# One more quantum between copy and transposes in two key chains of the second mixer, and one more quantum of projection ahead of its first scores

## The chip, the cores and the metric

The kernel runs on one core of a Trainium2 chip. TensorE (PE) does matmuls and transposes, VectorE (DVE), ScalarE (ACT) and GpSimd (POOL) the elementwise work, and SyncE (SP) issues the transfers. Each engine works through its own queue in order. The metric is the device time of one execution in microseconds, as the median of several runs.

## The reference, cut to what matters

The reference is a decoder trunk of two layers on 256 tokens of width 1024. Layer 0 has a mixer of a state-space part and a short convolution, layer 1 a mixer of attention; each layer ends in a mixture of experts. The change is in layer 1's mixer, of which this is the part that matters:

```python
proj = rms_norm(h) @ w_in                       # 2340 columns
qm, km, vm, qd, kc, vc, ks, vs, kw, vw, gl = split(proj)
# MoBA: 4 heads, one block of 256 keys: causal attention of qm on km, vm
# NSA: 12 heads in 2 groups, three branches on the queries qd:
k_cmp = rms_norm(compress_blocks(kc, ...))      # blocks of 32 tokens, stride 16: 15 keys
v_cmp = compress_blocks(vc, ...)                # gelu(flat @ w1) @ w2
o_c = softmax(qd @ k_cmp) @ v_cmp               # compressed branch
o_s = softmax(qd @ ks) @ vs                     # selected branch
o_w = softmax(qd @ kw) @ vw                     # window branch
o_nsa = g[0] * o_c + g[1] * o_s + g[2] * o_w
out = concat(o_moba, o_nsa) @ w_out
```

With 256 tokens all blocks are selected and the window holds every token.

## The kernel before

The order of the work on each engine is written out by hand: an instruction stands in its engine's queue where the program emits it. The function `odd` is the second mixer.

**The projection.** It is cut into nine pieces of 256 (one of 292) columns, and each piece into four quanta of 12 matmuls, numbered here q0 to q35 in the order in which they are emitted. Pieces come in the order 0, 1, 3, 2, 4, 5, 7, 6, 8. A quantum needs its weights as a high and a low half, made two quanta ahead by `prep`: ACT copies the high half (L211), and DVE or POOL, as the string `OD_SPLIT` says, subtracts to get the low half (L212; POOL for q14, q15, q18 to q20 and from q23 on). The first four matmuls of a quantum need the high half alone, the next four the low half.

**The jobs.** When a piece is done, a generator for it is appended to `jobs`: `blocks(0)` behind q3, `keys(1)` behind q7, `queries(3)` behind q11, `plain_values(2)` behind q15, `queries(4)` behind q19, and so on. `quantum()` emits one quantum (while there are some) and then calls `work()`, which moves each job on by one `yield`. So a `yield` in a job is a distance of one quantum in the queues.

- `blocks(0)` has ACT copy the raw compressed keys and values, scaled by `rs`, to `kd` (L962); at the next step it transposes them on PE (L969) and DVE adds the position terms into `fl` (L974).
- `keys` and `queries` begin with `head_rms`: squares on ACT (L868), the sum `hss` on DVE (L869), a chain of 16 small operations on POOL to `hrs` (L870 to L872), and some quanta later `hn` on DVE (L887 or L916), transposes on PE (L895 or L923) and the split results `kS`, `kmS` or `qS` (L901 and L902, L926 and L928).
- `compressed` follows 64 matmuls (L1172) on `fl`, in which `work()` is called four times: gelu (L978), transposes (L982), a matmul (L987), then a chain on POOL to `crs`; after two yields DVE makes `kn` (L995), after one more PE transposes it (L998) and spreads the values (L1001), and DVE and ACT finish `kcS` and `vpad` (L1005 to L1008). Then it goes on as `batch(3)`, whose scores are L1030, with L1033 and L1034 on DVE behind them.

**The attention.** It has 22 units u. A loop over i from -3 to 22 emits in this order: T(i), S(i+3), C(i+1), M(i+3), E(i+2), Q, V(i-1), D. S are the scores (L1091, L1094), M the maxima on DVE (L1100), E the exponentials on ACT (L1107), C the scaling on DVE (L1115 to L1126), T the transposes of probabilities (L1133, copied by L1134), V the values (L1154, L1160) with the split of the result into `yh` and `yl` (L211, L212). Units 0 to 17 are six groups of three, of which the middle one has no V; units 18 to 21 have two each. Q is one quantum (three in i = -3), and only a call of `work()` once all 36 are emitted. D is one unit of the output projection (L407, its weights L397 and L398): eight units are emitted in this half, the n-th of them after V has finished group n. The output projection is created at the end of the first iteration in which all quanta are emitted and no job is left.

Ahead of this loop q0 to q2 are emitted with the transposes of the input, then `quanta(9)` emits q3 to q11, then come the matmuls L1172, and `quanta(4)` emits q12 to q15. The three quanta of i = -3 are q16 to q18, and q35 is in i = 14.

Of the kernel before, what the change touches and what calls it, by code (L numbers as in the profile page):

```python
# [65 lines left out]
def tile_trunk(ctx: ExitStack, tc: tile.TileContext, x, cst, sml, s5c, ev_w_in, ev_w_out, od_w_in, od_w_out,  # L66
# [9 lines left out]
    def ps(tag, shape, dt=F32):  # L76
        return psum.tile(shape, dt, name=tag, tag=tag, bufs={"acc": 3, "mm": 2, "tp": 2, "o": 1}[tag])
# [15 lines left out]
    def cs(n):  # L93
        o, w = _CST[n]
        return C[:, o:o + w]
# [74 lines left out]
    def rsq2(pool, y, v, shape, eng=None):  # L170

        e = eng or ve
        t = [pool.tile(list(shape), F32, name=f"rsq{i}_{len(shape)}_{shape[-1]}", bufs=2) for i in range(2)]
        e.tensor_scalar(y.bitcast(I32), v.bitcast(I32), -0.5, MAGIC, op0=OP.mult, op1=OP.add)
        e.tensor_scalar(t[0], v, -0.5, None, op0=OP.mult)
        for _ in range(3):
            e.tensor_tensor(t[1], y, y, op=OP.mult)
            e.tensor_tensor(t[1], t[1], t[0], op=OP.mult)
            if eng:
                e.tensor_scalar(t[1], t[1], 1.5, None, op0=OP.add)  # L180
                e.tensor_tensor(y, t[1], y, op=OP.mult)
            else:
                e.scalar_tensor_tensor(y, t[1], 1.5, y, op0=OP.add, op1=OP.mult)
# [595 lines left out]
    def odd():  # L779
        with tc.tile_pool(name="odd", bufs=1, reuse_waits="tile") as sp:  # L780
# [39 lines left out]
            def quantum():  # L820
                nonlocal nq
                if nq < 36:
                    q, nq = nq, nq + 1
                    i, c0 = order[q // 4], 2 * (q % 4)
                    prep(q + 2)
                    n = pieces[i][2]
                    if c0 == 0:
                        if n > 256:
                            acc[i] = [ps("acc", [P, 512])[:, :n] for _ in range(2)]
                        else:  # L830
                            p = ps("mm", [P, 2, 256])
                            acc[i] = [p[:, t] for t in range(2)]
                    wh, wl = W.pop(q)
                    for m, (a, b) in enumerate(((xh, wh), (xh, wl), (xl, wh))):
                        for k in range(2):
                            for t in range(2):
                                pe.matmul(acc[i][t], a[:, c0 + k, t * P:(t + 1) * P], b[:, k],  # L837
                                          start=(c0 + k == 0 and m == 0 and (n > 256 or t == 0)),
                                          stop=(c0 + k == 7 and m == 2), skip_group_check=True)
                    if c0 == 6:  # L840
                        jobs.append(after[i])
                work()

            def quanta(n):
                for _ in range(n):
                    quantum()
# [113 lines left out]
            def blocks(i):  # L960
                for t in range(2):
                    ac.activation(kd[:, t], heads(acc[i][t])[:, :, None, :].to_broadcast([P, 4, 2, 64]), AF.Copy,  # L962
                                  scale=rs[:, t:t + 1])
                yield
                for i in range(2):
                    p = ps("tp", [P, 2, 2, P])
                    for hd in range(2):
                        for t in range(2):
                            pe.transpose(p[:, hd, t], kd[:, t, 2 * i + hd].rearrange("p a d -> p (a d)"), ident)  # L969
                    for r in range(2):  # L970
                        v = p[half[r]]
                        iv = bass.AP(tensor=v.tensor, offset=v.offset + r, ap=[v.ap[0], [2, 16], [256, 2], [16, 15]])
                        o = fl[half[r], i].rearrange("p s (h n) -> p s h n", h=2)[:, :, :, 0:15]
                        tt(o, iv, pev[half[r], i, :, None, None].to_broadcast([64, 16, 2, 15]), op=OP.add)  # L974
                    yield

            def compressed(ph):
                ac.activation(hid, ph, AF.Gelu_apprx_tanh)  # L978
                yield
                p = ps("tp", [P, 2, P])  # L980
                for c in range(2):
                    pe.transpose(p[:, c], hid[:, c * P:(c + 1) * P], ident)  # L982
                ve.tensor_copy(hT, p)
                yield
                p = ps("tp", [P, P])
                for c in range(2):
                    pe.matmul(p, hT[:, c], w2c[:, c].rearrange("p i n -> p (i n)"), start=(c == 0), stop=(c == 1))  # L987
                ac.activation(kc, p, AF.Copy)
                css, crs, sq = T("css", (P, 1)), T("crs", (P, 1)), T("csq", (P, 64), tag="hn", bufs=3)
                ac.activation(sq, p[:, 0:64], AF.Square, accum_out=css)  # L990
                po.tensor_scalar(css, css, 1.0 / 64, EPS, op0=OP.mult, op1=OP.add)
                rsq2(sp, crs, css, (P, 1), po)
                for _ in range(2):
                    yield
                ts(kn, kc[0:64, None, 0:64].to_broadcast([64, 2, 64]), crs[0:64], None, op0=OP.mult)  # L995
                yield
                p = ps("tp", [P, 512])
                pe.transpose(p[:, 0:64], kn.rearrange("p c d -> p (c d)"), ident[0:64, 0:64])  # L998
                rep = cs("rep").rearrange("p (h m) -> p h m", h=2)
                for hd in range(2):  # L1000
                    pe.matmul(p[0:96, 128 + 128 * hd:256 + 128 * hd], rep[:, hd], kc, start=True, stop=True,  # L1001
                              skip_group_check=True)
                v = p[:, 0:64].rearrange("p (h n) -> p h n", h=2)[:, :, 0:16]
                o = kcS[:, 0:64].rearrange("p (h m n) -> p h m n", h=2, m=2)
                ac.activation(o[:, :, 0], v, AF.Copy, scale=gkc)  # L1005
                stt(o[:, :, 1], v, gkc, o[:, :, 0].bitcast(F32), op0=OP.mult, op1=OP.subtract)
                for hd in range(2):
                    tt(vpad[:, hd], p[0:96, None, 192 + 128 * hd:256 + 128 * hd].to_broadcast([96, 6, 64]),  # L1008
                       cs("bm")[0:96, :, None].to_broadcast([96, 6, 64]), op=OP.mult)
                yield  # L1010
                yield from batch(3)
# [125 lines left out]
            def values(u):  # L1137
# [19 lines left out]
                if t == 1:  # L1157
# [6 lines left out]
                    ready.add(g)  # L1164

            after.update({0: blocks(0), 1: keys(1), 7: keys(7), 2: plain_values(2), 8: plain_values(8)})
            after.update({i: queries(i) for i in (3, 4, 5, 6)})
            quanta(9)
            ph = ps("o", [P, 256])
            for j in range(16):  # L1170
# [3 lines left out]
                if j % 4 == 3:  # L1174
                    work()
            jobs.append(compressed(ph))
            quanta(4)
            yh = big.tile([P, 8, 256], F32R, name="yh")
            yl = big.tile([P, 8, 256], F32R, name="yl")
            dense, nd = None, 0  # L1180
# [443 lines left out]
    even()  # L1624
    moe(0, False)
    odd()
    moe(1, True)

# [94 lines left out]
```

## Time and profile before

| | |
|---|---|
| median of 3 runs | 515.37 us (514.63 to 515.45) |
| profiled execution, its own time | 516.22 us |
| its span, first to last instruction | 514.6 us |
| busy: PE / DVE / ACT / POOL | 483.6 / 293.4 / 212.7 / 138.4 us |
| mean granted clock of PE, share of full speed | 0.991 |
| second mixer in the trace | about 244 to 387 us |

The profile is of one execution. Busy times add up instructions of an engine, overlapping ones once. A line of a timeline has the start in us, the duration in us of so many merged instructions, engine, line of the program, operation, tiles (written <- read), shapes, the count, and in brackets the idle time ahead of it with what ended it.

### The profile page before, as it was taken

How to read it: one execution, taken by the hardware profiler on the slowest of the kernel's cores; microseconds unless marked ns; L12 is line 12 of the kernel's file. 1: busy time of each engine (PE TensorE's matmuls, PEld its weight loads, DVE VectorE, ACT ScalarE, POOL GpSimd, SP SyncE). 2: the span in 40 equal slices, each digit the busy share in tenths (PEclk: the TensorE clock that was granted, in tenths of full speed). 3: DMA queues.
4: the chain of work that ended last, by engine and by line, in shares of the span. 5: the costliest groups of instructions: out<-in, count | busy, mean ns of one | idle time of the engine just before them, and what ended most of it. 6: DMA issues, size and time to landing. Idle time of an engine off the chain costs nothing. (4 is left out here: it accounts for less than half of the span.)

```text
span 514.6 us, 9047 instructions
## 1 busy us (share of the span) xinstructions
PE 483.6 (94%) x3245; PEld 324.7 (63%) x3245; DVE 293.4 (57%) x682; ACT 212.7 (41%) x468; POOL 138.4 (27%) x292
## 2 busy tenths in 40 slices
PE   7998998998989999999899889989998989999996
PEld 5997987786444443535877768877776444443532
DVE  6876678747733333435654687977547732333433
ACT  4636633664231121114645776786654131121211
POOL 6899980001000000010344556651232000000000
PEclk9999997999999999999999999999999999999998
DMA  8948942449599999999939600242059699999952
GB/s 295 406 157 335 405 162 84 144 154 323 179 400 384 358 417 413 419 385 383 317 130 377 222 0 3 91 159 80 1 163 415 265 378 384 348 414 414 407 248 82
DMA packets 36591, 137.63 MB, mean 267 GB/s; under 512 B 4544, under 2 KB 8768, under 8 KB 31424
## 3 DMA queue, kind: packets, MB, share of 16 engines
q1 hardware_dynamic: 36544, 137.03, 70.1%
q8 instruction: 27, 0.44, 0.3%
q14 instruction: 20, 0.16, 0.1%
HBM read 135.70 MB, written 1.05 MB: 266 GB/s over the span
## 5 line engine op out<-in xcount | busy, mean ns | idle before, releaser
L1482 PE MATMUL mm<-slab,xg 128*64 128x512 f32 (+1 forms) x512 | 99.2, 595 | 0.0
L1482 PEld LDWEIGHTS mm<-slab,xg 128*64 128x64 f32 (+1 forms) x512 | 30.5, 130 | 58.3 <-issue 55.4
L212 DVE TENSOR_TENSOR w<-slab,w 128x1024 fp32r<-128x1024 f32 (+2 forms) x39 | 39.9, 1031 | 13.4 <-ACT w L211 12.3
L313 PE MATMUL mm<-xh,w 128*128 128x256 f32 x288 | 41.3, 294 | 3.8 <-DVE yb L372 3.3
L1499 DVE COPY aT<-tp 128x256 f32<-128x256 f32 x14 | 5.9, 424 | 66.9 <-PE tp L1497 66.9
L211 ACT ACTIVATE w<-slab 128x512 fp32r<-128x512 f32 (+2 forms) x57 | 43.3, 780 | 1.3 <-PE mm L837 0.9
L313 PEld LDWEIGHTS mm<-xh,w 128*128 128x128 f32 x288 | 38.2, 201 | 4.1 <-issue 4.1
L837 PE MATMUL mm<-w,xh 128*128 128x256 f32 x256 | 38.6, 293 | 0.2 <-ACT xh L242 0.2
L837 PEld LDWEIGHTS mm<-w,xh 128*128 128x128 f32 x256 | 33.3, 189 | 1.2 <-ACT xh L242 0.9
L1488 ACT ACTIVATE si<-mm,rsl 128x256 f32<-128x256 f32 x14 | 6.7, 475 | 65.0 <-PE mm L1482 64.9
L1523 DVE TENSOR_TENSOR h<-h,acc 128x512 f32<-128x512 f32 x44 | 28.2, 681 | 2.8 <-PE acc L1520 2.8
L1511 PE MATMUL o<-slab,aT 128*64 128x512 f32 (+1 forms) x128 | 27.1, 603 | 1.0 <-DVE aT L1499 1.0
L849 POOL MEMSET fl<- 128x2048 f32 x1 | 1.8, 1804 | 97.1 <-PE tp L1423 97.1
L212 POOL TENSOR_TENSOR w<-slab,w 128x512 fp32r<-128x512 f32 (+1 forms) x18 | 24.0, 1339 | 13.9 <-ACT w L211 9.5
L1429 ACT ACTIVATE xg<-tp,sml 128x256 f32<-128x256 f32 (+1 forms) x32 | 12.6, 444 | 36.0 <-PE tp L1423 36.0
L212 DVE TENSOR_TENSOR ylp<-o,xlp 128x512 fp32r<-128x512 f32 x14 | 9.7, 692 | 30.4 <-ACT xlp L211 30.4
L1511 PE MATMUL acc<-slab,aT 128*64 128x512 f32 (+1 forms) x128 | 26.9, 600 | 0.0
L407 PE MATMUL acc<-w,yh 128*128 128x512 f32 x80 | 25.6, 399 | 0.0
L211 ACT ACTIVATE xlp<-o 128x512 fp32r<-128x512 f32 x14 | 8.4, 598 | 40.1 <-PE acc L1520 27.9
L1423 PEld LDWEIGHTS tp<-Pm,xhm 128*128 128x128 f32 x128 | 16.4, 189 | 11.1 <-issue 4.9
L398 DVE TENSOR_TENSOR w<-slab,w 128x512 fp32r<-128x512 f32 (+1 forms) x18 | 17.1, 964 | 10.4 <-ACT w L397 8.7
L1107 ACT ACTIVATE pr<-acc,mx 128x128 f32<-128x128 f32 (+1 forms) x56 | 22.9, 424 | 0.1
(436 smaller groups left out, 998.6 us busy)
## 6 DMA issues: line engine op xcount, KB each, us to landing
slab<-in_w_gate_dram SPq DMA_DIRECT2D x64, 512.0 KB, 8.1
slab<-in_w_up_dram SPq DMA_DIRECT2D x64, 512.0 KB, 8.9
slab<-in_w_down_dram SPq DMA_DIRECT2D x32, 1024.0 KB, 10.6
slab<-in_ev_w_in_dram SPq DMA_DIRECT2D x8, 1024.0 KB, 14.0
slab<-in_od_w_in_dram SPq DMA_DIRECT2D x8, 1024.0 KB, 6.6
slab<-in_ev_w_out_dram SPq DMA_DIRECT2D x4, 1024.0 KB, 12.3
slab<-in_od_w_out_dram SPq DMA_DIRECT2D x4, 1024.0 KB, 9.2
slab<-in_ev_w_in_dram SPq DMA_DIRECT2D x4, 512.0 KB, 7.5
```

The source lines that it names most:

```text
L211: ac.activation(hi, src, AF.Copy)
L212: (eng or ve).tensor_tensor(lo, src, hi.bitcast(F32), op=OP.subtract)
L313: pe.matmul(p, a[:, c], b[:, c], start=(c == 0 and n == 0), stop=(c == 7 and n == 2))
L398: (po if s.done in s.pool else ve).tensor_tensor(wl, v[:, o:o + s.n], wh.bitcast(F32), op=OP.subtract)
L407: pe.matmul(acc[t, f], a[:, c, t * P:(t + 1) * P], b[:, f * 512:(f + 1) * 512], start=(first and m == 0), stop=(last and m == 2))
L837: pe.matmul(acc[i][t], a[:, c0 + k, t * P:(t + 1) * P], b[:, k], start=(c0 + k == 0 and m == 0 and (n > 256 or t == 0)), stop=(c0 + k == 7 ...
L1107: ac.activation(pr[:, q * nk:(q + 1) * nk], U[u]["s"][:, q * w:q * w + nk], AF.Exp, bias=U[u]["m"][:, q:q + 1], accum_out=su[:, q:q + 1])
L1423: pe.matmul(p[b][:, d], v[:, t, c], Pm[:, t, 256 * g:256 * g + n_], start=(n + d + t == 0), stop=(n + t == 2), skip_group_check=True)
L1429: ac.activation(xgs[g][:, c, :n_], p[b][:, d], AF.Copy, scale=w)
L1482: pe.matmul(p[w * k:w * k + w], xgs[j // 2][:, c, o:o + w], wgu[j][k][c // 4][:, :, c % 4], start=(c == 0), stop=(c == 7), tile_position=( ...
L1511: pe.matmul(py[v], aT[:, c, v], wd[j][k][:, c, f * 512:(f + 1) * 512], start=(c == 0), stop=(c == 1), tile_position=(0, w * k))
L1523: tt(v, v, q[t], op=OP.add)
```

## The change

Three numbers of yields or quanta change, and nothing of the computation. `blocks` yields twice between the `kd` copies and the transposes, so that q5 stands between q4 and the first transposes instead of following them. `compressed` yields three times instead of twice ahead of `kn`. `quanta(5)` emits q12 to q16 ahead of the loop instead of q12 to q15; the three quanta of i = -3 are then q17 to q19, each later quantum stands one iteration of the loop earlier, and q35 is in i = 13.

```diff
@@ blocks
                     ac.activation(kd[:, t], heads(acc[i][t])[:, :, None, :].to_broadcast([P, 4, 2, 64]), AF.Copy,
                                   scale=rs[:, t:t + 1])
                 yield
+                yield
                 for i in range(2):
                     p = ps("tp", [P, 2, 2, P])
@@ compressed
                 rsq2(sp, crs, css, (P, 1), po)
-                for _ in range(2):
+                for _ in range(3):
                     yield
                 ts(kn, kc[0:64, None, 0:64].to_broadcast([64, 2, 64]), crs[0:64], None, op0=OP.mult)
@@ odd
             jobs.append(compressed(ph))
-            quanta(4)
+            quanta(5)
```

## Rows read from the trace of the kernel before

**Rows 1.** The page: busy time, share and instructions of each engine

```profile
PE 483.6 (94%) x3245; PEld 324.7 (63%) x3245; DVE 293.4 (57%) x682; ACT 212.7 (41%) x468; POOL 138.4 (27%) x292
```

**Rows 2.** Table of stretches: length, busy PE, PEld, DVE, ACT, POOL, clock, DMA

```profile
358.00:377.00 19.00, 19.00 (x121) 14.19 (x120) 11.38 (x28) 11.30 (x33) 5.27 (x4) 1.00 0.00 1
```

**Rows 3.** PE's waits, 244 to 377 us: in total, times, longest

```profile
PE tp L1133 <- DVE pr L1122: 1.7, 2, 1.0
PE tp L969 <- ACT early L962: 1.5, 2, 1.3
PE tp L998 <- DVE early L995: 1.4, 1, 1.4
PE tp L1133 <- DVE kmS L902: 1.3, 1, 1.3
PE tp L923 <- DVE hn L916: 1.0, 2, 0.6
...
PE tp L1133 <- DVE pr L1126: 0.6, 1, 0.6
...
PE tp L895 <- DVE hn L887: 0.3, 1, 0.3
```

**Rows 4.** Timeline of PE: the starts of q7 and q8

```profile
256.49 1.11 PE L837 MATMUL mm<-w,xh 128*128 128x256 f32 x8
...
257.91 1.11 PE L837 MATMUL mm<-w,xh 128*128 128x256 f32 x8
```

**Rows 5.** Timelines of ACT, DVE and POOL, 251 to 273 us

```profile
251.49 1.27 ACT L962 ACTIVATE early<-mm,rs 128x512 f32<-128x512 f32 x2 [2.57 <-POOL rs L181]
...
253.31 0.69 DVE L212 TENSOR_TENSOR w<-slab,w 128x512 fp32r<-128x512 f32 x1 [3.03 <-ACT w L211]
253.92 1.32 DVE L974 TENSOR_TENSOR fl<-tp,sml 64x480 f32<-64x480 f32 x2
...
258.98 0.69 DVE L869 TENSOR_REDUCE hss<-sq 128x8 f32<-128x512 f32 x1 [0.34 <-ACT sq L868]
259.58 1.96 DVE L212 TENSOR_TENSOR w<-slab,w 128x512 fp32r<-128x512 f32 x3
...
259.76 0.56 POOL L870 TENSOR_SCALAR hss<-hss 128x8 f32<-128x8 f32 x1 [7.73 <-DVE hss L869]
...
265.13 0.20 POOL L872 TENSOR_TENSOR hrs<-hrs,rs 128x8 f32<-128x8 f32 x1
268.14 0.20 POOL L870 TENSOR_SCALAR hss<-hss 128x8 f32<-128x8 f32 x1 [2.81 <-DVE hss L869]
...
272.38 0.20 POOL L872 TENSOR_TENSOR hrs<-hrs,rs 128x8 f32<-128x8 f32 x1
```

**Rows 6.** Timelines of POOL, DVE and ACT, 285 to 294 us

```profile
285.46 2.49 POOL L212 TENSOR_TENSOR w<-slab,w 128x512 fp32r<-128x512 f32 x2
...
285.54 1.26 DVE L995 TENSOR_SCALAR early<-early,crs 64x128 f32<-64x128 f32 x1 [2.14 <-POOL crs L181]
...
288.66 1.28 ACT L1107 ACT_TABLE_LOAD   x1
...
291.34 0.64 ACT L211 ACTIVATE w<-slab 128x512 fp32r<-128x512 f32 x1
292.59 0.84 ACT L868 ACTIVATE sq<-mm,rs 128x256 f32<-128x256 f32 x2 [0.61 <-PE mm L837]
```

**Rows 7.** Timelines of PE, ACT and DVE around the last values

```profile
373.29 0.66 PE L1154 MATMUL o<-pT,vm 128*64 128x128 f32 x8
373.87 0.50 PE L407 MATMUL mm<-w,yh 128*128 128x512 f32 x1
374.21 0.40 PE L407 MATMUL mm<-w,yl 128*128 128x512 f32 x1
...
373.99 0.39 ACT L211 ACTIVATE yh<-o 128x256 fp32r<-128x256 f32 x1 [1.38 <-PE o L1154]
...
374.41 0.42 DVE L212 TENSOR_TENSOR yl<-o,yh 128x256 fp32r<-128x256 f32 x1 [1.07 <-ACT yh L211]
```

## The prediction

> **What bounds the kernel now.** I read the page first, then the list of PE's waits cut to the second mixer's stretch, then tables of stretches, then the timelines of PE, ACT, DVE and POOL. PE is busy for 94% of the span [rows 1], so what can be won lies in the gaps of PE's in-order queue, and those are few. From 358 to 377 us PE is busy for the whole stretch [rows 2]: there the mixer is set by PE's own work, and any new wait costs its full length. The gaps lie further ahead, and the list of PE's waits names them [rows 3]: 1.5 us in two pieces before the transposes of L969 (for ACT's `kd` copies), 1.4 us before L998 (for DVE's `kn`), 1.7 us in two pieces and 0.6 us before the transposes of probabilities L1133, 1.3 us before one more of those (for `kmS`), 1.0 us in two pieces before L923, and 0.3 us before L895. No matmul is added or removed by the change, so its worth is the sum of these gaps now, less their sum afterwards. One quantum of the projection is 1.42 us of PE, the distance between the starts of two of them [rows 4].
>
> **First edit: a yield more in `blocks`.** Now PE reaches the transposes right after quantum q4, while ACT's `kd` copies start only at 251.49 us and take 1.27 us, because `rs` comes from POOL [rows 5]. With the yield q5 stands between, and its 1.42 us cover nearly all of the 1.5 us. But the mixer does not get these 1.5 us. What is late next is DVE. From 253.31 us its queue holds the low halves of the weights of q6 to q9 and the two pairs of additions L974. In rows: 253.31 to 253.92 is 0.6 for a low half, a pair of L974 is 1.32 [rows 5]; four low halves and two pairs make 4 x 0.65 + 2 x 1.32 = 5.3 us, whatever their order, so that the reduction `hss` of the first keys can start at 253.31 + 5.3 = 258.6 us, against 258.98 now [rows 5]. That is 0.35 us earlier and no more. The start of the queue does not move, since its first low half hangs on ACT's split behind the same `kd` copies. Behind `hss` comes POOL's chain to `hrs`, from 259.76 to 265.33 us [rows 5], then L895, and then the same chain for the first queries (268.14 to 272.58) and L923. PE has waits of 0.3 and 0.4 us there [rows 3], so both are set by that chain, and PE coming earlier only makes them longer. I take 0.35 us. The bounds: 0, if ACT's squares, not DVE, set the start, and 1.5, if the chain shrinks as well.
>
> POOL's first chain takes 5.57 us and the second 4.44 us. The first runs beside three low halves on DVE (from 259.58 us, 1.96 us) and its first operation takes 0.56 us; the same operation of the second takes 0.20 us [rows 5]. The Trainium skill (GPSIMD Engine Reference, section Specifications) says that GpSimd shares its SBUF interfaces with VectorE and is disturbed by VectorE's instructions with two SBUF inputs, and the trace agrees with that. By the order of the queue the low halves of q10 to q12 still follow `hss` directly, so the chain stays at 5.57 us and the term at 0.35; if they fell outside of it, 265.33 would come 1.1 us sooner and the term would be 0.35 + 1.1 = 1.45 us.
>
> **Second edit: three yields before `kn`, and quanta(5).** These belong together. The compressed keys keep their place against the units of attention (`kn` in the first of three quanta of i = -3), and there is one quantum more, q16, between the matmul L987 and `kn`. The 1.44 us before L998 lie between the end of q17 and the end of `kn`, which ran from 285.54 for 1.26 us, after POOL's chain to `crs` [rows 6]. With q18 in between they are covered. What is late next is the low half of q18's weights: POOL starts it at 285.46 us, when the chain is through, and does two in 2.49 us [rows 6], so it is there at 286.7. PE would be at q18 at about 285.5 and do its first four matmuls in 0.5 us, so it waits some 0.75 us for the fifth. Left of 1.4 are 0.65 us. The bounds are 0 (POOL later, or `kn` stretched further) and 1.4.
>
> **Third: the projection is one iteration ahead of the attention.** All jobs of the pieces from the fourth on run one iteration earlier. The squares of `queries(4)` on ACT (L868, 0.84 us) are now at 292.59, after the exponentials of unit 0, which with their table load take from 288.66 to 291.34 [rows 6]. With the change they come before them, and the exponentials wait for the end of q19. From there the path to the first transposes of probabilities, T0, is 0.84 for the squares, 2.7 for the exponentials, 0.64 for the split behind them [rows 6], then on DVE 0.65 for that split's low half and by my estimate 1.6 for `batch(3)`'s maxima and the scaling: 6.4 us. PE has two quanta and the matmuls of `batch(3)` and of two units for this time, which I estimate at 5.4. So T0 waits about 1.0 us where it waits 0.7 now (the 1.7 in two pieces, less the longest, 1.0). Against this `hn` of `queries(4)`, on which DVE sits until POOL is ready, moves out of the way of the next units, and the 0.6 and the 1.0 us before L1133 [rows 3] go. In their place I count 0.5 us before T1 (DVE's scaling behind `hn`) and 0.9 before `batch(4)`'s matmuls (they need the `qS` that DVE has only just finished). Now 0.7 + 0.6 + 1.0 = 2.3, afterwards 1.0 + 0.5 + 0.9 = 2.4: I take 0. The bounds: a loss of 1.8 (the rival below), a gain of 1.5 if two of the three do not come.
>
> The gaps of 0.6 (the second piece of L923's 1.0) and 1.3 us late in the mixer hang on POOL's chain for `queries(6)` and then on DVE's queue. The PE work between the end of q31 and that point is the same units' work in another order, so they stay; DVE has one 0.42 us `yl` less in front of `hss`, so I take a gain of 0.2, with bounds of a loss of 0.7 and a gain of 1.3.
>
> **What it costs at the end.** The last quantum is now in iteration 14 and goes to 13. Iteration 14 then has only T, S and no values on PE, some 1.05 us; DVE is ahead there by little, so 0.1 us, bounds 0 and 0.6. The output projection starts at iteration 15, and its last unit inside the loop becomes unit 7, directly behind the last values, V21, whose split it reads. Now unit 6 stands between. V21 starts at 373.29, `yh` is there at 374.38, `yl` at 374.83 [rows 7]. Unit 7 could start behind V21 at 373.87, but gets `yh` at 374.38: 0.5 us. Its second matmul, 0.34 us after the first (373.87 to 374.21), needs `yl`: 0.1 us more. So 0.6 us are lost where PE has no gap now [rows 2]; bounds 0.4 and 1.1.
>
> **Sum.** Gains 0.35 + 0.65 + 0 + 0.2 = 1.2 us, losses 0.1 + 0.6 = 0.7 us: a gain of 0.5 us. The profiled execution took 516.22 us, 1.6 us around its span of 514.6; it would become 515.7. It lies 0.85 us above the median of the runs, 515.37, so the median becomes 514.9. Behind the mixer the layer follows in a chain of PE, and a gain carries through.
>
> **The rivals.** *The stalls do go* (faster): POOL is less late than I count. If POOL's first chain is 1.1 us shorter, or the low half of q18 is there in time (0.75 more), or the waits before T1 and `batch(4)` stay away (up to 1.4), the gain grows from 0.5 by some 1.4 us, one of these or parts of two, to 1.9: 513.5 us. For it speaks that PE's 2.9 us before L969 and L998 are what the edits aim at and that both are covered by a quantum; against it that DVE and POOL stand on a continuous queue right behind each. Chance 0.37.
>
> *DVE blocks behind POOL in front of the first units* (slower): `hn` of `queries(4)` stands in DVE's queue one iteration earlier, before the scaling of unit 1. Such a chain on POOL takes 4.44 or 5.57 us [rows 5]. If it takes the longer time or more there, T1 and then `batch(4)` each wait about 0.9 us more than I count. This makes 0.5 - 1.8 = a loss of 1.3: 516.7 us. For it speaks that now, too, PE waits for L916 behind POOL before L923; against it that the scaling of unit 0 stays ahead of it. Chance 0.19.
>
> *The change does not do what it says*: `kn` still late behind q18, because POOL's chain grows by what now runs beside it. Then 0.65 falls away and the result is 515.5, still within the bound below; I count it with the forecast.
>
> **How the numbers follow.** A measurement of this kernel can tell about 0.2%, 1.0 us, from no change. Forecast, with the third rival: 0.44, and this is the chance of no change that can be told (514.4 to 516.4 us). Faster 0.37, slower 0.19, by the two rivals. The likeliest case alone spans 514.4 to 516.0 us. The range of 8 in 10 reaches to both outer cases: 513.3 to 516.6 us; all lower bounds together (a loss of 3) or all upper ones (a gain of 5) would need several mishaps at once.
>
> **What would show it.** Right: no wait before L969 over 0.4 us, but more than 1 us before L895 for `hn`; no wait before L998, but one of 0.5 to 1 us in front of q18's fifth matmul for POOL's `w`; a new wait of about 0.6 us before L407 after the last L1154. Wrong: L895 without a long wait (then the first edit brought its 1.5 us), no POOL wait at q18, or PE gaps of more than 1 us before T1 and L1030. A different PE clock, or a wait for a DMA in the mixer, would break the sum altogether.

## The result, and the profile after

The change made the kernel slower: a median of 521.04 us (519.78 to 521.15) beside 515.2 us (514.63 to 515.45) for the kernel before, a ratio of 1.0099 [1.0082, 1.0116]. The prediction was 514.9 us with a range to 516.6; slower by over 0.2% had a chance of 0.19. The two medians by themselves lie 5.84 us apart (1.0113) and the two profiled executions 3.56: three of the four executions of the new kernel, 521.00 to 521.15 us, had a mean granted clock of 0.984 to 0.989, the profiled one 0.996. The profiled execution of the new kernel is its fastest, 519.78 us with a span of 518.1, against 516.22 and 514.6 before. From L969 on its line numbers are larger by one.

The second mixer is best measured inside the trace, from the start of q4 to the first matmul of the gather that follows it (L1424; L1423 before): 248.14 to 399.17 us after, 249.35 to 395.63 us before. That is 151.03 against 146.28 us, a loss of 4.75 us; q4 itself starts 1.21 us sooner, since of the two profiled executions that of before had a stretch of half clock ahead of the mixer (0.50 from 80 to 84 us). Between points at which the same work is done (from the scores of `batch(3)` to T13 the new kernel has one quantum more behind it at each, 1.42 us by [rows 4], counted off) the 4.75 us divide like this:

| from q4 to | start before | start after | gained so far | in this step | predicted |
|---|---|---|---|---|---|
| first L923 | 273.19 | 271.53 | +0.45 | +0.45 | +0.35 |
| scores of `batch(3)` | 289.06 | 288.41 | +0.86 | +0.41 | +0.65 |
| T0 | 295.24 | 295.25 | +0.20 | -0.66 | |
| T4 | 312.44 | 311.80 | +0.85 | +0.65 | 0 for both |
| T13 | 347.89 | 352.17 | -4.07 | -4.92 | +0.2 |
| gather | 395.63 | 399.17 | -4.75 | -0.68 | -0.7 |

Up to T4 the forecast holds (1.0 us predicted, 0.85 measured), and from T13 to the end it holds too. All of the surprise lies between 312 and 352 us. PE's waits of the kernel after, 244 to 380 us (in total, times, longest), read against [rows 3]:

```profile
PE tp L1134 <- DVE kmS L902: 2.3, 1, 2.3
PE tp L1134 <- DVE pr L1123: 1.6, 2, 1.2
PE acc L1092 <- DVE sb L1034: 1.6, 2, 1.2
PE mm L837 <- POOL w L212: 1.4, 2, 0.8
PE tp L895 <- DVE hn L887: 0.9, 1, 0.9
...
PE tp L1134 <- DVE pr L1127: 0.5, 1, 0.5
PE mm L407 <- ACT yh L211: 0.5, 1, 0.5
PE tp L923 <- DVE hn L916: 0.4, 1, 0.4
...
PE tp L970 <- ACT early L962: 0.2, 1, 0.2
```

The two waits that the edits aim at are gone or small (L969's 1.5 us is 0.2, L998's 1.4 us has no line), and three expected ones stand there: 0.9 before L895, 0.8 for POOL's `w` at q18, 0.5 before L407. Not foreseen are the second wait for `w`, 0.63 us at q26, and the 2.3 us before a unit's transposes. POOL and DVE of the kernel after show where the first of these comes from:

```profile
302.61 1.40 POOL L212 TENSOR_TENSOR w<-slab,w 128x512 fp32r<-128x512 f32 x1 [3.31 <-ACT w L211]
307.92 0.42 POOL L1023 MEMSET sc<- 128x384 f32 x1 [3.90 <-PE tp L1058]
308.42 0.20 POOL L870 TENSOR_SCALAR hss<-hss 128x8 f32<-128x8 f32 x1
...
312.66 0.20 POOL L872 TENSOR_TENSOR hrs<-hrs,rs 128x8 f32<-128x8 f32 x1
312.82 2.52 POOL L212 TENSOR_TENSOR w<-slab,w 128x512 fp32r<-128x512 f32 x2
...
314.15 2.62 DVE L1127 TENSOR_SCALAR pr<-pr,su 128x256 f32<-128x256 f32 x2
```

POOL stands 3.90 us in front of one memset, and everything queued behind it, the chain to `hrs` and q26's weights, comes late. And PE around T12, with the table of stretches for the same time (length, busy PE, PEld, DVE, ACT, POOL, granted clock, DMA share, GB/s):

```profile
339.72 0.66 PE L1134 MATMUL tp<-sml,pr 128*128 128x128 f32 x4
...
342.68 0.60 PE L895 MATMUL tp<-sml,hn 128*128 128x128 f32 x4
343.52 0.66 PE L923 MATMUL tp<-sml,hn 128*128 128x128 f32 x4 [0.25 <-ACT pcT L1060]
346.46 0.66 PE L1134 MATMUL tp<-sml,pr 128*128 128x128 f32 x4 [2.28 <-DVE kmS L902]
...
347.72 2.27 PE L837 MATMUL mm<-w,xh 128*128 128x256 f32 x8
```

```profile
340.00:344.00 4.00, 3.75 (x31) 3.19 (x29) 2.47 (x6) 3.15 (x8) 3.42 (x10) 1.00 0.12 45
344.00:348.00 4.00, 1.72 (x12) 1.44 (x10) 3.94 (x6) 2.17 (x5) 0.59 (x1) 0.90 0.54 171
348.00:352.00 4.00, 4.00 (x33) 3.54 (x31) 1.60 (x5) 0.86 (x4) 0.00 (x0) 0.68 0.26 93
```

The wait is not the whole cost. Behind it the granted clock falls from 2.4 to 1.2 GHz for a part of the next two stretches (0.90 and 0.68 in the mean), and eight matmuls that take 1.1 us in [rows 4] take 2.27. With one row of POOL and those of DVE the wait itself is read:

```profile
342.10 2.50 POOL L212 TENSOR_TENSOR w<-slab,w 128x512 fp32r<-128x512 f32 x2
...
342.17 0.76 DVE L916 TENSOR_TENSOR hn<-mm,hrs 128x256 f32<-128x256 f32 x2 [1.46 <-POOL hrs L872]
...
343.43 1.72 DVE L1123 TENSOR_TENSOR pr<-pr,su 128x512 f32<-128x512 f32 x1
345.07 0.68 DVE L1101 TENSOR_REDUCE mx<-acc 128x2 f32<-128x512 f32 x1
345.67 0.73 DVE L902 SCALAR_TENSOR_TENSOR kmS<-tp,sml,kmS 128x512 fp32r<-128x512 f32 x1
```

There are two `tp` buffers in PSUM. L895 writes one, L923 the other, T12 the first again, which L902 has to have read; and L902 is queued on DVE behind `hn` of `queries(6)`, which waits for POOL. That is not all of it: between the two the scaling L1123 takes 1.72 us beside the two low halves that POOL starts as soon as `hrs` is through; in e9_wait2 below, where it runs ahead of `hn`, it takes 0.69. These 1.03 us are a good part of the 2.28. In the kernel before the pair L1126 is lengthened in the same way (at 344.99, 1.58 us long; undisturbed such a pair takes 0.62).

### The profile page after: what moved, and what is told of

It is laid out like the page before. It is cut to its first block, busy times and chain, and to the rows that moved or that the text cites. A ratio compares the mean times of both kernels' runs of the same rounds, so it can differ in the third digit from the quotient of the medians.

```text
span 518.1 us, 9048 instructions
## 1 busy us (share of the span) xinstructions
PE 484.6 (94%) x3245; PEld 323.6 (62%) x3245; DVE 296.4 (57%) x682; ACT 212.7 (41%) x468; POOL 136.4 (26%) x292
## 5 line engine op out<-in xcount | busy, mean ns | idle before, releaser
L212 DVE TENSOR_TENSOR w<-slab,w 128x1024 fp32r<-128x1024 f32 (+2 forms) x39 | 40.0, 1034 | 14.7 <-ACT w L211 13.6
L313 PE MATMUL mm<-xh,w 128*128 128x256 f32 x288 | 39.6, 285 | 4.2 <-DVE yb L372 3.3
L837 PE MATMUL mm<-w,xh 128*128 128x256 f32 x256 | 40.3, 298 | 1.7 <-POOL w L212 1.4
L313 PEld LDWEIGHTS mm<-xh,w 128*128 128x128 f32 x288 | 36.3, 191 | 4.7 <-issue 4.7
L212 POOL TENSOR_TENSOR w<-slab,w 128x512 fp32r<-128x512 f32 (+1 forms) x18 | 23.7, 1327 | 13.6 <-ACT w L211 8.3
L212 DVE TENSOR_TENSOR ylp<-o,xlp 128x512 fp32r<-128x512 f32 x14 | 9.7, 692 | 30.4 <-ACT xlp L211 30.4
L407 PE MATMUL acc<-w,yh 128*128 128x512 f32 x80 | 25.8, 401 | 0.5 <-DVE w L398 0.5
L1424 PEld LDWEIGHTS tp<-Pm,xhm 128*128 128x128 f32 x128 | 16.4, 189 | 11.1 <-issue 4.9
```

The costliest lines, as they stand in the source:

```text
L212: (eng or ve).tensor_tensor(lo, src, hi.bitcast(F32), op=OP.subtract)
L313: pe.matmul(p, a[:, c], b[:, c], start=(c == 0 and n == 0), stop=(c == 7 and n == 2))
L407: pe.matmul(acc[t, f], a[:, c, t * P:(t + 1) * P], b[:, f * 512:(f + 1) * 512], start=(first and m == 0), stop=(last and m == 2))
L1424: pe.matmul(p[b][:, d], v[:, t, c], Pm[:, t, 256 * g:256 * g + n_], start=(n + d + t == 0), stop=(n + t == 2), skip_group_check=True)
```

## The experiments

Each ratio is to executions of the kernel before from the same session. Beside it stands the mixer in the profiled execution as measured above: its length (to within 0.05 us), PE's busy and idle time in it, and the stretches of 4 us in it whose clock was under 0.97. The last column adds up (1 - clock) x 4 us over these, the time that PE loses to the clock if it is busy all through.

| kernel | ratio to before | length | PE busy | idle | clock falls at | clock's cost |
|---|---|---|---|---|---|---|
| before | 1 | 146.28 | 135.25 | 11.03 | none | 0 |
| after | 1.0099 | 151.03 | 138.19 | 12.84 | 344: 0.90, 348: 0.68 | 1.7 |
| e1_sc2 | 1.0050 | 149.27 | 137.71 | 11.56 | 344: 0.71, 348: 0.86 | 1.7 |
| e2_blocks | 0.9990 | 147.30 | 137.10 | 10.20 | 308: 0.57 | 1.7 |
| e3_quanta5 | 1.0118 | 152.90 | 139.77 | 13.13 | 296, 300, 320, 324, 348 | 5.0 |
| e4_yields3 | 1.0077 | 151.38 | 138.89 | 12.49 | 308: 0.54, 312: 0.61 | 3.4 |
| e5_sc2_wait2 | 0.9983 | 145.65 | 136.06 | 9.59 | none | 0 |
| e6_dense_later | 0.9975 | 145.11 | 135.90 | 9.21 | none | 0 |
| e7_blocks_wait2 | 0.9970 | 144.57 | 135.24 | 9.33 | none | 0 |
| e8_yields3_sc2 | 1.0052 | 149.52 | 137.02 | 12.50 | 292: 0.68, 296: 0.89 | 1.7 |
| e9_wait2 | 1.0029 | 147.32 | 136.52 | 10.80 | none | 0 |
| e10_control | 0.9976 | 146.26 | 136.84 | 9.42 | 308: 0.60 | 1.6 |
| e11_wait4 | 1.0084 | 150.75 | 138.25 | 12.50 | 344: 0.89, 348: 0.68 | 1.7 |
| e12_all | 0.9997 | 146.56 | 136.49 | 10.07 | none | 0 |

**The memset: a second buffer for `sc`.** `batch(3)` and `batch(4)` use one buffer `sc`, and `batch` clears it on POOL before filling it. e1_sc2 is the kernel after with another buffer for `batch(4)`.

```diff
-                sc = T("sc", (P, 2, 2, 6, 16))
+                sc = big.tile([P, 2, 2, 6, 16], F32, name="sc4", tag="junk") if i == 4 else T("sc", (P, 2, 2, 6, 16))
```

> The changed kernel with a second buffer for the tile sc of batch(4), so that POOL's memset of it no longer waits for batch(3)'s transposes. Theory A (the loss comes from POOL standing 3.9 us in front of that memset, because batch(3) is now a quantum later against the queries): the wait goes, the chain to hrs starts at about 306 us instead of 308.4, the wait of PE for POOL's w at q26 and most of the waits at T5 to T9 go, and the median falls by 2 to 3 us to 518 to 519. Theory B (the loss comes from the jobs of the projection standing one iteration earlier against the attention, where DVE is full): within 0.5 us of the changed kernel, 520.5 to 521.5.

Measured 1.005 [1.0035, 1.0066]: about half of the loss is gone. POOL and DVE of e1_sc2:

```profile
304.25 0.41 POOL L1023 MEMSET sc<- 128x384 f32 x1
306.38 0.20 POOL L870 TENSOR_SCALAR hss<-hss 128x8 f32<-128x8 f32 x1 [1.72 <-DVE su L1116]
...
311.28 0.20 POOL L872 TENSOR_TENSOR hrs<-hrs,rs 128x8 f32<-128x8 f32 x1
311.43 2.52 POOL L212 TENSOR_TENSOR w<-slab,w 128x512 fp32r<-128x512 f32 x2
...
314.01 0.62 DVE L1127 TENSOR_SCALAR pr<-pr,su 128x256 f32<-128x256 f32 x2
```

The memset no longer waits, `hrs` is there 1.4 us sooner and q26 has its weights. T12's 2.3 us and the clock fall behind it remain.

**The parts of the change alone, each in the kernel before.** e2_blocks has only the second yield of `blocks`, e3_quanta5 only `quanta(5)`, e4_yields3 only the three yields, and e8_yields3_sc2 these with the second `sc` buffer.

```diff
 e2_blocks
                 yield
+                yield
 e3_quanta5
-            quanta(4)
+            quanta(5)
 e4_yields3, e8_yields3_sc2
-                for _ in range(2):
+                for _ in range(3):
                     yield
```

> The kernel before with the second yield in blocks alone. Both theories: 0.3 to 0.5 us faster than before, about 514.8; the 1.5 us before L969 fall to 0.3, and L895 waits 0.8 us or more for hn.

> The kernel before with quanta(5) alone, two yields before kn. batch(3) keeps its distance from the queries, so the memset of sc does not wait. Theory A: near the kernel before, 515 to 516.5 (0.6 us lost at the last unit of the output projection, kn still waits). Theory B: the iteration is what counts, 518 to 520.

> The kernel before with three yields before kn alone, quanta(4). batch(3) is a quantum later against queries(4), so the memset of sc waits for its transposes; the projection keeps its iterations. Theory A: POOL waits about 3 us at L1022 and the median is 516 to 518, though the wait before kn goes. Theory B: no loss, 514 to 515.

> The kernel before with three yields before kn and a second buffer for sc, quanta(4). Against the kernel with three yields alone (3.5 us slower than before) this takes only POOL's wait of 7.8 us before the memset away. Theory A: 3 to 5 us faster than that kernel, at or below the kernel before. Theory B (batch(3) an iteration later, with its DVE work among the first units, is what costs): still 2 us or more slower than the kernel before.

e2_blocks came out at 0.999 [0.9976, 1.0004], with waits of 0.2 before L970 and 0.8 before L895: the first edit does what the prediction says, with neither gain nor loss that can be told. (Its mixer is the longer one in the profile because the clock fell there, for 1.7 us; PE is idle for 0.83 us less.) e3_quanta5 is the slowest kernel of all, 1.0118 [1.009, 1.0147], worse than its theory B (518 to 520 us; the median is 522.06), though it has no wait for `sc`: the memset is not needed for a loss of this size. PE's waits of it, and its table of stretches:

```profile
PE tp L1133 <- DVE kmS L902: 2.3, 1, 2.3
PE tp L1133 <- DVE pr L1122: 2.1, 1, 2.1
...
PE tp L1133 <- ACT qS L926: 1.4, 1, 1.4
```

```profile
296.00:300.00 4.00, 3.43 (x19) 3.33 (x20) 3.86 (x11) 2.28 (x7) 3.02 (x6) 0.70 0.00 0
...
320.00:324.00 4.00, 2.94 (x15) 2.79 (x16) 3.84 (x9) 3.85 (x10) 0.17 (x1) 0.69 0.63 208
...
348.00:352.00 4.00, 3.47 (x16) 3.29 (x17) 3.60 (x8) 1.62 (x5) 0.00 (x0) 0.60 0.78 254
```

Three waits of units' transposes, and the clock falls behind each. PE is idle for only 2.10 us more than before, but busy for 4.52 us more with the same matmuls, and the clock's 5.0 us cover that. e4_yields3, 1.0077 [1.0056, 1.0099], has the memset's wait at its largest:

```profile
POOL sc L1022 <- PE tp L1057: 7.8, 1, 7.8
```

A second buffer there (e8_yields3_sc2, 1.0052 [1.0038, 1.0065]) won back 0.25%, which is its theory B and not the 3 to 5 us of A: idle time stays at 12.5 us, with waits of 2.9 us in all for `sb` (2.2 in e4_yields3) and 1.6 for `pr` (0.9). So neither the second edit nor `quanta(5)` can be had by itself. That the two together win something, as the prediction says, no run shows: in the kernel after they stand together and lose, and with every mend (e6_dense_later, below) they are no faster than e7_blocks_wait2, which has neither.

**T12: `hn` of `queries(6)` one quantum later.** `OD_WAIT` gives the yields between a chain's start and its `hn`. e9_wait2 changes it for `queries(6)` in the kernel after, e5_sc2_wait2 does so in e1_sc2, e7_blocks_wait2 in e2_blocks, and e10_control is e7_blocks_wait2 with the second `sc` buffer.

```diff
-OD_WAIT = {1: 3, 3: 3, 4: 2, 5: 3, 6: 1, 7: 3}
+OD_WAIT = {1: 3, 3: 3, 4: 2, 5: 3, 6: 2, 7: 3}
```

> The changed kernel with the second buffer for sc and one more yield in queries(6) (OD_WAIT[6] from 1 to 2), so that its hn, on which DVE waits for POOL, stands behind the scaling of unit 12 instead of ahead of it. Theory A (the 2.3 us before T12, and the PE clock that falls behind them, come from hn blocking DVE): both go, and the median falls by 2 to 3.5 us against the kernel with the second sc buffer, to about 515.5 where the kernel before takes 515.8. Theory B (T12 waits for its PSUM bank whatever DVE's order, or the clock falls anyway): less than 0.7 us.

> The kernel before with the second yield in blocks and one more yield in queries(6). Theory A: the waits of 0.6 us before L923 and 1.3 us before T13 go, 1.5 to 2 us faster than the kernel before, about 514. Theory B: the waits move to the next iteration, within 0.5 us of the kernel with the second yield in blocks alone.

> The changed kernel with one more yield in queries(6) alone, one buffer for sc. If the late wait and its clock fall are a share of the loss of their own: 3 to 3.5 us faster than the changed kernel, 1.003 to 1.005 of the kernel before, with POOL's wait before the memset of sc still there. If the late wait was only a result of POOL's earlier delay: it stays, and the ratio stays near 1.01.

> A control: the kernel before with the second yield in blocks and the longer wait of queries(6), and the second buffer for sc. There the memset does not wait for batch(3), so by theory A the buffer changes nothing: within 0.3 us of that kernel, ratio 0.997. If the buffer helps by something else, as a place or a shorter wait of another engine, it is over 1 us faster.

e9_wait2 measured 1.0029 [1.0015, 1.0042] against 1.0099 for the kernel after. Its PE, DVE and stretches at the same place:

```profile
342.88 0.60 PE L895 MATMUL tp<-sml,hn 128*128 128x128 f32 x4
343.73 0.66 PE L1134 MATMUL tp<-sml,pr 128*128 128x128 f32 x4 [0.25 <-ACT pcT L1060]
...
341.25 0.69 DVE L1123 TENSOR_TENSOR pr<-pr,su 128x512 f32<-128x512 f32 x1
...
344.95 0.74 DVE L916 TENSOR_TENSOR hn<-mm,hrs 128x256 f32<-128x256 f32 x2
```

```profile
344.00:348.00 4.00, 4.00 (x43) 3.71 (x43) 2.86 (x8) 2.77 (x8) 1.36 (x2) 1.00 0.38 107
348.00:352.00 4.00, 4.00 (x36) 3.09 (x32) 3.46 (x10) 3.58 (x13) 0.00 (x0) 1.00 0.43 158
```

T12 no longer stands behind L923, `hn` comes after it, and the clock stays at 1.00. The mixer is 3.71 us shorter: 2.04 of idle time and 1.67 of busy time, and the second is just the clock's 1.7. The memset's wait of 3.9 us is still there in e9_wait2, so the two causes are separate: with both mended, e5_sc2_wait2 is at 0.9983 [0.9972, 0.9995]. In the kernel without the change the same edit of `OD_WAIT` wins too: e7_blocks_wait2 is at 0.997 [0.9957, 0.9982]; of the 1.96 us in two waits that stood there before (0.63 and 1.33) one of 1.04 us is left. e10_control, 0.9976 [0.9963, 0.9989], shows that a second `sc` buffer without the crossing does nothing that can be told.

**The end, and another way to mend the memset.** e6_dense_later is e5_sc2_wait2 with the output projection created one iteration later, as in the kernel before. e11_wait4 is the kernel after with `hn` of `queries(4)`, and so `batch(4)`, one quantum later; e12_all has that with the two other mends and no second buffer.

```diff
 e6_dense_later, e12_all
-                if nq == 36 and not dense and not jobs:
+                if nq == 36 and i > 14 and not dense and not jobs:
 e11_wait4
-OD_WAIT = {1: 3, 3: 3, 4: 2, 5: 3, 6: 1, 7: 3}
+OD_WAIT = {1: 3, 3: 3, 4: 3, 5: 3, 6: 1, 7: 3}
 e12_all
+OD_WAIT = {1: 3, 3: 3, 4: 3, 5: 3, 6: 2, 7: 3}
```

> The same as the kernel with the second sc buffer and the longer wait of queries(6), and the output projection is created an iteration later, so that unit 6 stands between V21 and unit 7 again. Theory A (the 0.5 us before L407 for yh and what follows it are the whole price at the end): 0.5 to 0.75 us faster than that kernel, and no wait before L407. Theory B (iteration 15 then has no work to cover T16, and the price comes back there): within 0.3 us.

> The changed kernel with one more yield in queries(4) (OD_WAIT[4] from 2 to 3), one buffer for sc. batch(4) then begins behind batch(3)'s transposes again, as in the kernel before, so the memset of sc does not wait long. Theory A: as with the second buffer, 2 to 3 us faster than the changed kernel, ratio 1.004 to 1.006. If the second buffer helped by something else: no gain, ratio 1.009 or more.

> The changed kernel with one more yield in queries(4) and one in queries(6), and the output projection created an iteration later. Theory A: all three causes gone without a second buffer, ratio 0.996 to 0.998, like the kernel that has the second buffer in place of the longer wait of queries(4) (0.9975). If the waits move on behind queries(4): 1.000 or more.

e6_dense_later measured 0.9975 [0.9963, 0.9987] and has no wait before L407; its mixer is 0.54 us shorter than that of e5_sc2_wait2, about the 0.6 us that the prediction charged, though the two intervals overlap. e11_wait4 was a miss, 1.0084 [1.0065, 1.0102]: POOL no longer waits at the memset, but PE gets waits of 0.3 to 0.6 us in its place (0.6 for ACT's `pr` before L1031, 0.4 for `hn` in front of a quantum), and T12 starts at 346.49 us, where it did in the kernel after. e12_all came out at 0.9997 [0.9983, 1.0011], worse than e6_dense_later for the same reason. Of the two ways to undo the crossing, only the buffer adds no wait.

The fastest version, faster than both kernels, is e7_blocks_wait2, and e6_dense_later, which has all three edits and every mend, is not faster. Its PE is idle as long (9.21 and 9.33 us). So with the new waits removed, what the second and third edits win and lose comes to nothing.

## Why the prediction was wrong

**First edit, as predicted.** 0.45 us gained of the 1.5 aimed at (0.35 predicted); DVE's queue and POOL's chain took the rest, as the 0.85 us before L895 show, a little less than the "more than 1 us" that was to be the sign of it.

**Second edit, nearly.** The wait for `w` at q18 is 0.80 us (0.75 predicted) and 0.41 us were gained (0.65). The difference is q18 itself: the wait cuts its first eight matmuls into pieces of 0.63 and 0.74 us, 0.27 us more than the 1.10 that they take in one.

**Third edit, the start: right in the sum, not in the parts.** T0 waits 1.15 us (1.0 predicted), T1 not at all (0.5), `batch(4)`'s scores 0.21 and 0.27 (0.9), but L1092 waits 1.23 for `sb`, which I had not counted. The sum over T0 to T4 was put at 0 and measured at -0.01.

**Missed altogether: the memset.** The step "Third: the projection is one iteration ahead of the attention" counts ACT, DVE and PE, and not what `batch(4)` itself issues. The second edit delays `batch(3)`, the third advances `batch(4)`: in the kernel before, PE did `batch(3)`'s transposes of `sc` at 305.00 us, directly ahead of `batch(4)`'s scores at 305.35, and POOL's memset at 306.62 found the buffer free. After, the scores of `batch(4)` are at 301.11 and the transposes of `batch(3)` at 307.25, and the memset of the one waits for the other. First the rows before, then those after:

```profile
305.00 0.60 PE L1057 MATMUL tp<-sml,sc 128*96 128x128 f32 x4
305.35 1.12 PE L1030 MATMUL acc<-kcS,qS 128*128 128x192 f32 x8
...
306.62 0.42 POOL L1022 MEMSET sc<- 128x384 f32 x1
```

```profile
301.11 0.69 PE L1031 MATMUL acc<-kcS,qS 128*128 128x192 f32 x4 [0.21 <-DVE qS L928]
...
307.25 0.60 PE L1058 MATMUL tp<-sml,sc 128*96 128x128 f32 x4
```

Counting every instruction of the moved step would have found it: POOL's part is the memset L1022, and its buffer has a reader in the other job. Its price is 1.8 us in the traces (151.03 less 149.27), 0.49% between the ratios and 2.5 us between the medians.

**The step that failed by its own words** is that for the gaps "late in the mixer": the same units' work in another order, "so they stay". They hang on the order. Before, the values V(11) stand between L923 and T13, 1.5 us of PE work (L1154 at 345.03 to the end of L1160 at 346.56), and split the wait for POOL's chain and DVE into 0.63 and 1.33 us:

```profile
344.32 0.79 PE L923 MATMUL tp<-sml,hn 128*128 128x128 f32 x4 [0.63 <-DVE hn L916]
345.03 1.09 PE L1154 MATMUL o<-pT,vsw 128*64 128x128 f32 x16
345.96 0.60 PE L1160 MATMUL o<-pcT,vpad 96*64 96x256 f32 x4
347.89 0.66 PE L1133 MATMUL tp<-sml,pr 128*128 128x128 f32 x4 [1.33 <-DVE kmS L902]
```

With `queries(6)` one iteration earlier, V(10) would stand there, but unit 10 is the middle one of its group and has no V. The two pieces became 0.25 and 2.28 us, 0.6 us more. That is within the bounds of the prediction (a loss of 0.7).

**What had no price at all is the clock.** The prediction says that another clock would break the sum and gives no price for it. Behind the 2.28 us the clock fell, at a cost of 1.67 us, measured as the difference in PE's busy time between the kernel after and e9_wait2. So a wait that grew by 0.6 us cost 2.3. The clock alone does not make the miss: without the late wait and its clock fall e9_wait2 is still at 1.0029, and without the memset's wait e1_sc2 at 1.0050, where the range ended at 1.0024 of the prediction's 515.37 us; only with both mended does the time lie inside. The prediction's lower bounds, besides, add up to a loss of 1.8 + 0.7 + 0.6 + 1.1 = 4.2 us and not to the 3 that it names; the 4.75 us lie beyond that as well.

**The rival that I gave 0.19** is slower, as the result is, but by another way: DVE was to block behind POOL before T1, and T1 doesn't wait. The mechanism that it describes (`hn` on DVE in front of a unit's scaling, waiting for POOL) is that of T12, 50 us later.

**The end, as predicted:** 0.48 us before L407, and 0.68 in all from T13 on (0.7).

Of the 4.75 us, then, 1.8 are the memset, 0.6 and 1.67 the wait before T12 with its clock, and 0.7 the end: together 4.8, set against a gain of 0.85 up to T4. About 0.8 us remain. They are two waits between T4 and T12, where the kernel before has none:

```profile
320.18 0.63 PE L1134 MATMUL tp<-sml,pr 128*128 128x128 f32 x4 [0.47 <-DVE pr L1123]
...
331.93 0.63 PE L1134 MATMUL tp<-sml,pr 128*128 128x128 f32 x4 [0.37 <-ACT sb L1042]
```

In e1_sc2 both are still there with 0.39 us each, and in e9_wait2 with 0.46 and 0.38, so neither the memset nor T12 makes them; which of the moved jobs does, no experiment says. PE is besides busy for 0.7 to 1.3 us longer than before with all three edits, even where the clock stays at 1.00 (e5_sc2_wait2, e6_dense_later, e9_wait2). That goes with the number of its waits from 244 to 380 us, 13 before and 15, 14 and 17 in these: as at q18, the pieces on both sides of a wait are longer together than the run that it cuts.

## What to carry to other kernels

When an edit moves two jobs against each other, list for each the scratch buffers that they share and the first instruction that writes one: on an in-order queue a wait of that instruction is a wait of everything behind it. When a step is called "the same work in another order", write out what stands between the late result and its reader in the new order, unit by unit, since some units have less work than others. And price a PE wait at more than its length: at some 0.25 us more where it cuts a run of matmuls in two, and here at 1.7 us more where it was one of 2.3 us.

## What the hardware showed that I had not expected

A clock fall followed the 2.3 us before a unit's transposes in all four profiles that have it (after, e1_sc2, e3_quanta5, e11_wait4), each costing 1.6 to 1.7 us. Behind shorter waits it is not fixed: e7_blocks_wait2 and e10_control list the same waits of PE to within 0.1 us, and only the second fell to 0.60 at 308 to 312 us, which made its mixer 1.7 us longer. The Trainium skill (TensorE: Matmul & The Clock Gate, Part 1) says that a gate halves the engine's clock when it has been idle and opens again when it is busy. The 0.90 and 0.68 behind T12, and the 1.00 at 352 to 356 us, agree with it.

POOL's weight operation also slows DVE's scaling beside it. Behind the memset's wait the pair L1127 took 2.62 us with POOL's L212 running, from 312.82 us on, and 0.62 us in e1_sc2, where the two L212 had ended at 313.95; ahead of T12 it was L1123 with 1.72 us, and 0.69 in e9_wait2. The Trainium skill (GPSIMD Engine Reference, section Specifications) says that the two engines share their SBUF interfaces, and that GpSimd contends there with VectorE's instructions that run in a 2-port mode or have two inputs from SBUF. The trace agrees for L1123, which multiplies `pr` by `su`, by a factor of 2.5; the factor is four for the pair L1127, of which no run tells the mode.
